# Attention scores of the first query block as one product for both halves of the keys, and the mask added on VectorE

## The chip, the cores and the metric

The kernel runs on one core of one Trainium2 chip. The metric is the device time of one execution in microseconds (us); less is better. The median of three runs of the kernel before is 2488.39 us.

## The reference

Two layers of a streaming encoder work on 256 frames of width 2048. Layer 0 mixes tokens with a gated spatial MLP, layer 1 with latent attention of 16 heads; behind each stands a gated MLP with a short causal convolution. The change is in the attention of layer 1. Queries come in blocks of 128, and a block reads keys up to its own end. A frame sees keys of its own chunk of 64 frames and of earlier ones:

```python
for qb in range(S // Q_BLOCK):
    q0 = qb * Q_BLOCK
    k_end = q0 + Q_BLOCK
    s = (jnp.einsum('bqhd,bkhd->bhqk', q_nope[:, q0:k_end], k_nope[:, :k_end])
         + jnp.einsum('bqhr,bkr->bhqk', q_rope[:, q0:k_end], k_rope[:, :k_end]))
    s = s.astype(jnp.float32) * SM_SCALE
    allowed = (kpos[None, :] // CHUNK) <= (qpos[:, None] // CHUNK)
    s = jnp.where(allowed[None, None], s, -jnp.inf)
    p = jax.nn.softmax(s, axis=-1).astype(v.dtype)
    outs.append(jnp.einsum('bhqk,bkhd->bqhd', p, v[:, :k_end]))
```

So the first block has scores of 128 queries by 128 keys, the second of 128 by 256. In each, the first 64 queries of the block must not see the last 64 of its keys.

## The kernel before

**Precision by halves.** TensorE multiplies rounded operands (type fp32r). For the precision of fp32 each operand is split into a rounded part, called high, and the rest, called low. ScalarE makes the high part (a cast: `wh` of a weight, line 127, `hi` of an activation), VectorE the low part (a subtraction: `wl`, line 130). A product is then high x high + low x high + high x low, added up in a PSUM bank. The class `Feed` loads weights in chunks of 128x2048 by DMA from SyncE's queue and splits them ahead of their use; its casts stand on ScalarE and VectorE between all other work.

**One head, in three steps.** `attend_a` (line 1059) makes the scores `sc` of one head in one PSUM bank: columns 0 to 127 for the first block of queries, 128 to 383 for the second. Per block there are five products: high queries by high keys, low queries by high keys, high queries by low keys (`knT`, `qnT`), and two of the rotary part (`krT`, whose two halves lie side by side, with `qrT`). The mask is an eleventh product: `negq` has -1e30 in row 0 for the first 64 queries, `keyr` has 1 in row 0 for the last 64 keys of each block, and their product, of 256 columns in bf16, adds -1e30 where a key is hidden. Then VectorE takes the maximum of each block (line 1079, out of PSUM) and scales it (1080), ScalarE takes the exponentials with their sums (1082), VectorE the reciprocal (1084) and the scaled probabilities `p` (1086).

`attend_b` (line 1089) transposes `p` in three products into `pt` (1094), and ScalarE copies it to `pts` (1096). `attend_c` (line 1099) multiplies by the values `vv` into `o` and splits that into `oT`: ScalarE the high part (1108), VectorE the low one (1109).

**The loop over heads** (lines 1135 to 1154) weaves these steps of three heads into the output projection `mo`. Heads 0 to 3 get their scores earlier, between the products that make `vv`. An iteration `t` has, on TensorE, the scores of head t; six `mo` products of 512 columns for the first 128 frames (`acc[0]`); the transposes of head t-1; three `mo` products; the values of head t-2; three more `mo` products. `mo` of iteration t uses the head `t - 4`.

**What sets the order.** Each engine runs its instructions in order and waits on semaphores of others. The Tile framework schedules: it may move an instruction past others of the same engine, so the order on an engine is not the source's. Eight PSUM banks are shared: four hold `mo`, four go around among `sc`, `pt` and `o`.

Of the kernel before, what the change touches and what calls it, by code (L numbers as in the profile page):

```python
# [8 lines left out]
F32 = mybir.dt.float32  # L9
F32R = mybir.dt.float32r  # L10
BF16 = mybir.dt.bfloat16
AF = mybir.ActivationFunctionType
ALU = mybir.AluOpType
AX = mybir.AxisListType

P = 128
S = 256
D = 2048
KD = D // P
# [5 lines left out]
H = 16  # L25
# [5 lines left out]
SM_SCALE = (NOPE + ROPE) ** -0.5  # L31
LN_EPS = 1e-5
RMS_EPS = 1e-6
NEG = -1.0e30
# [17 lines left out]
T1, T2 = 6, 5  # L52
# [161 lines left out]
def trunk(ctx: ExitStack, tc: tile.TileContext, x, xT, gm_in, gm_wout, ffn_up, ffn_dn,  # L214
          ml_q, ml_kv, ml_b, ml_out, consts, w_sT, b_s, ropes, ln_rows, out):
    nc = tc.nc

    cpool = ctx.enter_context(tc.tile_pool(name="cpool", bufs=1))
    big = ctx.enter_context(tc.tile_pool(name="big", bufs=1))
    tp = ctx.enter_context(tc.tile_pool(name="tp", bufs=3))  # L220
# [6 lines left out]
    def slot(shape, name, dt=F32, tag="big"):  # L227
        return big.tile(shape, dt, tag=tag, name=name, bufs=SLOTS[tag])
# [4 lines left out]
    def mm(o, l, r, start, stop):  # L233
        recent[0] = nc.tensor.matmul(o, l, r, start=start, stop=stop, skip_group_check=True)  # L234
# [70 lines left out]
    for j in range(4):  # L305
        t = slot([P, 4, S], f"xraw{j}", tag="side")
# [35 lines left out]
    nc.gpsimd.memset(epsc[:, 0:1], LN_EPS)  # L342
    nc.gpsimd.memset(epsc[:, 1:2], RMS_EPS)

    negq = cpool.tile([P, P], BF16, name="negq")
    nc.gpsimd.memset(negq, 0.0)
    nc.gpsimd.memset(negq[0:1, 0:64], NEG)
    keyr = cpool.tile([P, 2, P], BF16, name="keyr")
    nc.gpsimd.memset(keyr, 0.0)
    nc.gpsimd.memset(keyr[0:1, :, 64:P], 1.0)  # L350

    def rstd_of(var, eps, name):
        q = st.tile([P, 1], F32, tag="rstd", name=f"{name}q")
# [6 lines left out]
    def x_parts(xs, k, b):  # L360
        t = xs[k // 4]
        return (t[:, k % 4, b * P : (b + 1) * P], t[:, k % 4, S + b * P : S + (b + 1) * P])

    def prod_b(acc, parts, hi, lo, pieces, first, last):

        xh, xl = parts
        for f, (o, w) in enumerate(pieces):
            mm(acc[f][:, :w], xh, hi[:, o : o + w], first, False)
            mm(acc[f][:, :w], xl, hi[:, o : o + w], False, False)
            mm(acc[f][:, :w], xh, lo[:, o : o + w], False, last)  # L370
# [322 lines left out]
    halfp = [(0, 512), (512, 512)]  # L693
# [15 lines left out]
    for gi in range(6):  # L709

        acc = Banks(f"v{gi}", DIRECT if gi == 0 else DIRECT + OWN if gi % 2 else OWN + DIRECT)
# [23 lines left out]
        for i, (n, t) in enumerate(zip(DIRECT, rest)):  # L735
            o = vt[:, i // 2, (i % 2) * 512 : (i % 2) * 512 + 512]
# [75 lines left out]
    for gi in range(12):  # L812
        acc = [bank(f"u{gi}_{f}") for f in range(4)]
        for c in range(4):
            hi, lo = feed.next()
# [14 lines left out]
    acc, end = down(NF_GM, pT, "wo", ln, acts)  # L830
# [69 lines left out]
    ln, acc, end = ffn(0, ln, acc, end, False)  # L900
# [5 lines left out]
    krT = slot([P, 2, S], "krT", F32R)  # L906
# [55 lines left out]
    acc = [[bank(f"mkv{b}_{f}") for f in range(2)] for b in range(2)]  # L962
    for c in range(6):
        hi, lo = feed.next()
        for j in range(3 if c < 5 else 1):
            k = 3 * c + j
# [9 lines left out]
    for b in range(2):  # L976
# [3 lines left out]
        t = tp.tile([P, 4, ROPE], F32, tag="t1", name=f"kr2_{b}", bufs=T1)  # L980
# [13 lines left out]
    qrT = [slot([P, 8, S], f"qrT{i}", F32R) for i in range(2)]  # L994
# [4 lines left out]
    acc = [[bank(f"qr{b}_{f}") for f in range(2)] for b in range(2)]  # L999
    for c in range(2):  # L1000
        hi, lo = feed.next()
        for j in range(2):
            k = 2 * c + j
# [52 lines left out]
    oT = []  # L1056
    probs = {}

    def attend_a(h):

        q, k = qT[h // 4][:, h % 4, :], kT[h // 4][:, h % 4, :]
        sc = bank(f"sc{h}")
        mx = st.tile([P, 4, 2], F32, tag="mx", name=f"mx{h}")
        p = tp.tile([P, 3 * P], F32, tag="t2", name=f"p{h}", bufs=T2)
        cc = [slice(0, P), slice(P, 3 * P)]
        for b in range(2):
            nk = (b + 1) * P
            o = sc[:, cc[b]]

            qh, ql = q[:, b * P : (b + 1) * P], q[:, S + b * P : S + (b + 1) * P]  # L1070
            qr = qrT[h // 8][:, h % 8, b * P : (b + 1) * P]
            mm(o, qh, k[:, 0:nk], b == 0, False)
            mm(o, ql, k[:, 0:nk], False, False)
            mm(o, qh, k[:, S : S + nk], False, False)
            mm(o, qr, krT[:, 0, 0:nk], False, False)
            mm(o, qr, krT[:, 1, 0:nk], False, False)
        mm(sc.rearrange("p (n c) -> p n c", n=2)[:, :, 0:P], negq, keyr, False, True)
        for b in range(2):
            nc.vector.reduce_max(mx[:, 0, b : b + 1], sc[:, cc[b]], axis=AX.X)
        nc.vector.tensor_scalar(mx[:, 1, :], mx[:, 0, :], -SM_SCALE, None, op0=ALU.mult)  # L1080
        for b in range(2):
            nc.scalar.activation(p[:, cc[b]], sc[:, cc[b]], AF.Exp, bias=mx[:, 1, b : b + 1], scale=SM_SCALE,
                                 accum_out=mx[:, 2, b : b + 1])
        nc.vector.reciprocal(mx[:, 3, :], mx[:, 2, :])
        for b in range(2):
            nc.vector.tensor_scalar(p[:, cc[b]], p[:, cc[b]], mx[:, 3, b : b + 1], None, op0=ALU.mult)
        probs[h] = p
# [11 lines left out]
    def attend_c(h):  # L1099
        if h % 4 == 0:  # L1100
            oT.append(slot([P, 4, 512], f"oT{h // 4}", F32R))
        pts = probs.pop(h)
        o = bank(f"o{h}")
        c = slice(h * P, (h + 1) * P)
        mm(o[:, 0:S], vv[0][:, c], pts[:, 0:S], True, False)
        mm(o[:, P:S], vv[1][:, c], pts[:, S : 3 * P], False, True)
        hi = oT[h // 4][:, h % 4, 0:S]
        nc.scalar.copy(hi, o[:, 0:S])
        nc.vector.tensor_tensor(oT[h // 4][:, h % 4, S : 2 * S], o[:, 0:S], hi.bitcast(F32), ALU.subtract)  # L1109

    for hf in range(2):
        acc = [[bank(f"vv{hf}_{b}_{f}") for f in range(2)] for b in range(2)]
        for c in range(2):
            hi, lo = feed.next()
            for j in range(2):

                k = 2 * c + j
# [7 lines left out]
        for b in range(2):  # L1125
            for f in range(2):
                c = slice(hf * 1024 + f * 512, hf * 1024 + (f + 1) * 512)
# [4 lines left out]
    acc = [[bank(f"mo0_{b}_{f}") for f in range(2)] for b in range(2)]  # L1132
    LAG = 4
    attend_c(0)
    for t in range(3, H + LAG):
        k = t - LAG
        if k >= 0:
            if k % 2 == 0:
                hi, lo = feed.next()
            w = slice((k % 2) * 1024, (k % 2) * 1024 + 1024)  # L1140
        if 3 < t < H:
            attend_a(t)
        if k >= 0:
            prod_b(acc[0], x_parts(oT, k, 0), hi[:, w], lo[:, w], halfp, k == 0, k == KD - 1)
        if t == 3:
            attend_c(1)
        if t - 1 < H:
            attend_b(t - 1)
        if k >= 0:
            prod_b(acc[1][:1], x_parts(oT, k, 1), hi[:, w], lo[:, w], halfp[:1], k == 0, k == KD - 1)  # L1150
        if 3 < t < H + 2:
            attend_c(t - 2)
        if k >= 0:
            prod_b(acc[1][1:], x_parts(oT, k, 1), hi[:, w], lo[:, w], halfp[1:], k == 0, k == KD - 1)
    ln.begin()
# [4 lines left out]
    acc = [[bank(f"mo1_{b}_{f}") for f in range(2)] for b in range(2)]  # L1160
    late = []
    for c in range(8):
        left = 7 - c
        hi, lo = feed.next(splits=2 if left > 5 else 3, loads=2)
        for j in range(2):
            k = 2 * c + j
            w = slice(j * 1024, (j + 1) * 1024)
# [11 lines left out]
    ln, acc, end = ffn(1, ln, banks, end_mo, True)  # L1179
# [92 lines left out]
```

## Time and profile before

| what | value |
|---|---|
| median of 3 runs | 2488.39 us (2487.24 to 2489.69) |
| profiled execution | 2486.63 us |
| its span | 2484.8 us |
| TensorE busy | 2468.0 us, 99% |
| VectorE busy | 1992.9 us, 80% |
| ScalarE busy | 1424.6 us, 57% |
| scores of the 16 heads | between 1626 and 1709 us of the span |

The span is what the profiler saw between first and last instruction; the execution's own time is 1.8 us longer. PE is TensorE's matrix part, PEld its loads of weights, DVE is VectorE, ACT ScalarE, POOL GpSimd, SP SyncE. Matmuls overlap and their ends are modelled: how long one really costs is seen from its start to the start of the next.

### The profile page before, as it was taken

The page shows a single profiled execution, that of the slowest core. Times are in us where ns is not written, and L with a number is a line of the kernel's source. Part 1 is how long each engine was busy: PE and PEld are TensorE (multiplying, and loading weights), DVE is VectorE, ACT ScalarE, POOL GpSimd, SP SyncE. Part 2 cuts the span into 40 slices and gives each one's busy share as a digit, 9 for nine tenths or more (in the row PEclk, how much of TensorE's full clock was granted, in tenths as well). Part 3 has the DMA queues.
Part 4 walks back from the last instruction along what each step waited for, and adds up shares of the span by engine and source line. Part 5 has one row for each costly group of instructions (what it writes and reads, how often), then busy time and mean ns, then how long its engine had stood idle before and what let it go on. Part 6 is the DMA issues. An engine that isn't in the chain of part 4 may idle for free. (4 is left out here: it accounts for less than half of the span.)

```text
span 2484.8 us, 33520 instructions
## 1 busy us (share of the span) xinstructions
PE 2468.0 (99%) x12995; PEld 2122.3 (85%) x12995; DVE 1992.9 (80%) x2802; ACT 1424.6 (57%) x1979; POOL 89.0 (4%) x173
## 2 busy tenths in 40 slices
PE   9999999999999999999999999999999999999998
PEld 7888888888888888888888888988888888888886
DVE  7999866679898789787677897856598788768798
ACT  6676544446565756566554566655566656655453
POOL 0000000000000000000000000000001000000000
PEclk9999999999999999999999999999999999999999
DMA  7556544546665689788558885544489789647885
GB/s 280 203 206 223 198 173 169 185 170 214 209 203 203 218 349 351 286 335 315 188 198 319 302 305 185 182 155 151 174 294 347 293 333 341 238 155 286 299 325 199
DMA packets 108991, 606.17 MB, mean 244 GB/s; under 512 B 10272, under 2 KB 11040, under 8 KB 61600
## 3 DMA queue, kind: packets, MB, share of 16 engines
q1 hardware_dynamic: 84832, 463.51, 52.2%
q0 software_dynamic: 24000, 140.52, 14.7%
q8 instruction: 102, 1.67, 0.3%
q14 instruction: 57, 0.47, 0.1%
HBM read 538.98 MB, written 65.01 MB: 243 GB/s over the span
## 5 line engine op out<-in xcount | busy, mean ns | idle before, releaser
L130 DVE TENSOR_TENSOR wl<-raw,wh 128x1024 fp32r<-128x1024 f32 (+4 forms) x693 | 968.2, 1418 | 222.4 <-ACT wh L127 136.9
L127 ACT CAST wh<-raw 128x1024 fp32r<-128x1024 f32 (+4 forms) x693 | 820.2, 1211 | 388.0 <-PE u L234 84.6
L234 PE MATMUL up<-xhl,wh 128*128 128x512 f32 x2624 | 612.0, 390 | 0.9 <-ACT wh L127 0.9
L234 PEld LDWEIGHTS up<-xhl,wh 128*128 128x128 f32 x2624 | 487.3, 188 | 99.4 <-ACT wh L127 1.8
L234 PEld LDWEIGHTS up<-xhl,wl 128*128 128x128 f32 x2624 | 325.9, 192 | 7.2 <-DVE wl L130 0.7
L234 PE MATMUL up<-xhl,wl 128*128 128x256 f32 x2624 | 328.5, 283 | 0.5 <-DVE wl L130 0.5
L234 PE MATMUL u<-xhl,wh 128*128 128x512 f32 x768 | 184.7, 393 | 0.1
L234 PEld LDWEIGHTS u<-xhl,wh 128*128 128x128 f32 x768 | 141.0, 188 | 31.6 <-issue 3.8
L127 ACT CAST th<-ts 128x1536 fp32r<-128x1536 f32 x106 | 110.1, 1052 | 87.8 <-DVE ts L137 62.7
L130 DVE TENSOR_TENSOR tl<-ts,th 128x1536 fp32r<-128x1536 f32 x106 | 125.3, 1218 | 8.1 <-PE dn_p L234 3.4
L234 PEld LDWEIGHTS u<-xhl,wl 128*128 128x128 f32 x768 | 95.4, 192 | 2.0
L234 PE MATMUL u<-xhl,wl 128*128 128x256 f32 x768 | 96.0, 283 | 0.0
L234 PE MATMUL mo<-wh,oT 128*128 128x512 f32 x256 | 83.0, 404 | 0.0
L137 DVE TENSOR_TENSOR ts<-ts,raw 128x512 f32<-128x512 f32 x106 | 72.6, 685 | 0.9
L234 PE MATMUL v_q<-wh,xhl 128*128 128x512 f32 x224 | 69.2, 390 | 1.2 <-ACT wh L127 1.2
L137 DVE TENSOR_TENSOR ts<-raw 128x1024 f32<-128x1024 f32 x53 | 64.5, 1218 | 0.9 <-PE wo_q L234 0.7
L234 PE MATMUL v_p<-wh,xhl 128*128 128x512 f32 x192 | 59.8, 390 | 0.1
L234 PEld LDWEIGHTS mo<-wh,oT 128*128 128x128 f32 x256 | 45.4, 189 | 7.4 <-DVE oT L1109 0.2
L234 PEld LDWEIGHTS v_q<-wh,xhl 128*128 128x128 f32 x224 | 41.9, 188 | 10.7 <-ACT wh L127 2.1
L234 PE MATMUL mo<-wl,oT 128*128 128x512 f32 x128 | 50.2, 392 | 0.0
L686 ACT ACTIVATE lny<-lnt,lncol 128x128 f32<-128x128 f32 x96 | 36.6, 471 | 15.6 <-PE lnt L682 15.5
L171 DVE TENSOR_TENSOR pwl<-praw,pwh 128x1536 fp32r<-128x1536 f32 x16 | 28.1, 1755 | 20.4 <-ACT pwh L170 20.4
(1701 smaller groups left out, 4165.4 us busy)
## 6 DMA issues: line engine op xcount, KB each, us to landing
raw<-in_ffn_up_dram SPq DMA_DIRECT2D x172, 1024.0 KB, 6.4
raw<-in_gm_in_dram SPq DMA_DIRECT2D x93, 1024.0 KB, 4.8
raw<-in_ffn_dn_dram SPq DMA_DIRECT2D x68, 1024.0 KB, 6.8
raw<-in_gm_wout_dram SPq DMA_DIRECT2D x48, 1024.0 KB, 5.4
praw<-in_ffn_dn_dram POOLq DMA_DIRECT2D x16, 1024.0 KB, 14.8
keptth<-pth POOLq DMA_DIRECT2D x16, 1024.0 KB, 6.4
kepttl<-ptl POOLq DMA_DIRECT2D x16, 1024.0 KB, 8.8
fth<-keptth POOLq DMA_DIRECT2D x16, 1024.0 KB, 9.5
```

What stands on the lines that cost most here:

```text
L127: cast = self.nc.scalar.copy(hi, raw)
L130: self.nc.vector.tensor_tensor(lo, raw, hi.bitcast(F32), ALU.subtract)
L137: add = lambda o, a, b: self.nc.vector.tensor_tensor(o, a, b, ALU.add)
L171: pin(nc.vector.tensor_tensor(lo[:, 0:cols], raw[:, o : o + cols], hi[:, 0:cols].bitcast(F32), ALU.subtract))
L234: recent[0] = nc.tensor.matmul(o, l, r, start=start, stop=stop, skip_group_check=True)
L686: nc.scalar.activation(y[:, j], t[:, j * P : (j + 1) * P], AF.Identity, bias=lncol[:, o : o + 1], scale=lncol[:, g : g + 1])
```

## The change

For the first block of queries, three products take the place of five: high queries by high and low keys side by side in one product of 256 columns (a view of two blocks of 128), low queries by high keys (128 columns), and the rotary queries by both halves of the rotary keys (256 columns). The two halves of the result lie in columns 0 to 127 and 128 to 255; ScalarE copies the second to SBUF (`sl`, line 1079 of the changed kernel), and VectorE adds it to the first into `p` (1082). The second block of queries has the five products that it had, in columns 256 to 511. The mask product goes: VectorE adds a column `negc` (-1e30 in its first 64 rows) in place to the two hidden groups of 64 columns (1081). Maximum and exponential of the first block read `p` in SBUF instead of PSUM. In the loop, `attend_c` of head t-2 moves ahead of `attend_b` of head t-1, and that behind three more `mo` products.

```diff
--- before.py
+++ after.py
@@ -342,12 +342,9 @@
     nc.gpsimd.memset(epsc[:, 0:1], LN_EPS)
     nc.gpsimd.memset(epsc[:, 1:2], RMS_EPS)
 
-    negq = cpool.tile([P, P], BF16, name="negq")
-    nc.gpsimd.memset(negq, 0.0)
-    nc.gpsimd.memset(negq[0:1, 0:64], NEG)
-    keyr = cpool.tile([P, 2, P], BF16, name="keyr")
-    nc.gpsimd.memset(keyr, 0.0)
-    nc.gpsimd.memset(keyr[0:1, :, 64:P], 1.0)
+    negc = cpool.tile([P, 1], F32, name="negc")
+    nc.gpsimd.memset(negc, 0.0)
+    nc.gpsimd.memset(negc[0:64, :], NEG)
 
     def rstd_of(var, eps, name):
         q = st.tile([P, 1], F32, tag="rstd", name=f"{name}q")
@@ -1063,23 +1060,32 @@
         mx = st.tile([P, 4, 2], F32, tag="mx", name=f"mx{h}")
         p = tp.tile([P, 3 * P], F32, tag="t2", name=f"p{h}", bufs=T2)
         cc = [slice(0, P), slice(P, 3 * P)]
+        two = lambda t: t.rearrange("p (n c) -> p n c", n=2)
+        qh = lambda b: q[:, b * P : (b + 1) * P]
+        ql = lambda b: q[:, S + b * P : S + (b + 1) * P]
+        qr = lambda b: qrT[h // 8][:, h % 8, b * P : (b + 1) * P]
+
+        mm(two(sc[:, 0:S]), qh(0), two(k)[:, :, 0:P], True, False)
+        mm(sc[:, 0:P], ql(0), k[:, 0:P], False, False)
+        mm(two(sc[:, 0:S]), qr(0), krT[:, :, 0:P], False, False)
+        o = sc[:, S : 2 * S]
+        mm(o, qh(1), k[:, 0:S], False, False)
+        mm(o, ql(1), k[:, 0:S], False, False)
+        mm(o, qh(1), k[:, S : 2 * S], False, False)
+        mm(o, qr(1), krT[:, 0, :], False, False)
+        mm(o, qr(1), krT[:, 1, :], False, True)
+
+        lo = tp.tile([P, P], F32, tag="t1", name=f"sl{h}", bufs=T1)
+        nc.scalar.copy(lo, sc[:, P:S])
+        hidden = sc.rearrange("p (n c) -> p n c", c=64)[:, 1:8:6, :]
+        nc.vector.tensor_scalar(hidden, hidden, negc, None, op0=ALU.add)
+        nc.vector.tensor_tensor(p[:, cc[0]], sc[:, 0:P], lo, ALU.add)
+        src = [p[:, cc[0]], o]
         for b in range(2):
-            nk = (b + 1) * P
-            o = sc[:, cc[b]]
-
-            qh, ql = q[:, b * P : (b + 1) * P], q[:, S + b * P : S + (b + 1) * P]
-            qr = qrT[h // 8][:, h % 8, b * P : (b + 1) * P]
-            mm(o, qh, k[:, 0:nk], b == 0, False)
-            mm(o, ql, k[:, 0:nk], False, False)
-            mm(o, qh, k[:, S : S + nk], False, False)
-            mm(o, qr, krT[:, 0, 0:nk], False, False)
-            mm(o, qr, krT[:, 1, 0:nk], False, False)
-        mm(sc.rearrange("p (n c) -> p n c", n=2)[:, :, 0:P], negq, keyr, False, True)
-        for b in range(2):
-            nc.vector.reduce_max(mx[:, 0, b : b + 1], sc[:, cc[b]], axis=AX.X)
+            nc.vector.reduce_max(mx[:, 0, b : b + 1], src[b], axis=AX.X)
         nc.vector.tensor_scalar(mx[:, 1, :], mx[:, 0, :], -SM_SCALE, None, op0=ALU.mult)
         for b in range(2):
-            nc.scalar.activation(p[:, cc[b]], sc[:, cc[b]], AF.Exp, bias=mx[:, 1, b : b + 1], scale=SM_SCALE,
+            nc.scalar.activation(p[:, cc[b]], src[b], AF.Exp, bias=mx[:, 1, b : b + 1], scale=SM_SCALE,
                                  accum_out=mx[:, 2, b : b + 1])
         nc.vector.reciprocal(mx[:, 3, :], mx[:, 2, :])
         for b in range(2):
@@ -1142,14 +1148,12 @@
             attend_a(t)
         if k >= 0:
             prod_b(acc[0], x_parts(oT, k, 0), hi[:, w], lo[:, w], halfp, k == 0, k == KD - 1)
-        if t == 3:
-            attend_c(1)
+        if t < H + 2:
+            attend_c(t - 2)
+        if k >= 0:
+            prod_b(acc[1][:1], x_parts(oT, k, 1), hi[:, w], lo[:, w], halfp[:1], k == 0, k == KD - 1)
         if t - 1 < H:
             attend_b(t - 1)
-        if k >= 0:
-            prod_b(acc[1][:1], x_parts(oT, k, 1), hi[:, w], lo[:, w], halfp[:1], k == 0, k == KD - 1)
-        if 3 < t < H + 2:
-            attend_c(t - 2)
         if k >= 0:
             prod_b(acc[1][1:], x_parts(oT, k, 1), hi[:, w], lo[:, w], halfp[1:], k == 0, k == KD - 1)
     ln.begin()
```

What the scheduler makes of it. First a steady iteration on TensorE, with the scores of head 9. Before, its score products:

```order
L234 MATMUL sc_14726<-knT_14109,qnT_13809 128x128 x3
L234 MATMUL sc_14726<-krT,qrT_13464 128x128 x2
L234 MATMUL sc_14726<-knT_14109,qnT_13809 128x256 x3
L234 MATMUL sc_14726<-krT,qrT_13464 128x256 x2
L234 LDWEIGHTS negq
L234 MATMUL sc_14726<-keyr,negq 128x2x128
```

and now:

```order
L234 MATMUL sc_14732<-knT_14106,qnT_13806 128x256
L234 MATMUL sc_14732<-knT_14106,qnT_13806 128x128
L234 MATMUL sc_14732<-krT,qrT_13461 128x256
L234 MATMUL sc_14732<-knT_14106,qnT_13806 128x256 x3
L234 MATMUL sc_14732<-krT,qrT_13461 128x256 x2
```

Eleven products are eight. Behind the scores come, before and after, four rows of `mo_0` (six products). What follows these was:

```order
L1094 MATMUL pt_14754<-ident,p_14683 128x128 x3
L234 MATMUL mo_1_0_14457<-wh_14476,oT_14619 128x512 x2
L234 MATMUL mo_1_0_14457<-wl_14477,oT_14619 128x512
L234 MATMUL o_14763<-pts_14713,vv_13465 128x256
L234 MATMUL o_14763<-pts_14713,vv_13466 128x128
L234 MATMUL mo_1_1_14458<-wh_14476,oT_14619 128x512 x2
L234 MATMUL mo_1_1_14458<-wl_14477,oT_14619 128x512
```

and is now:

```order
L234 MATMUL o_14761<-pts_14727,vv_13462 128x256
L234 MATMUL o_14761<-pts_14727,vv_13463 128x128
L234 MATMUL mo_1_0_14458<-wh_14477,oT_14614 128x512 x2
L234 MATMUL mo_1_0_14458<-wl_14478,oT_14614 128x512
L1100 MATMUL pt_14769<-ident,p_14688 128x128 x3
L234 MATMUL mo_1_1_14459<-wh_14477,oT_14614 128x512 x2
L234 MATMUL mo_1_1_14459<-wl_14478,oT_14614 128x512
```

The values `o` of head 7 stood behind the transposes `pt` of head 8; now they stand ahead of them, and three `mo` products more stand ahead of `pt`. On ScalarE the same iterations (heads 8 and 9) had:

```order
L1108 CAST oT_14619<-o_14718 128x256
L1082 ACTIVATE p_14683,mx_14682<-sc_14681,mx_14682 128x128
L1082 ACTIVATE p_14683,mx_14682<-sc_14681,mx_14682 128x256
L1096 COPY pts_14713<-pt_14709 128x384
L1082 ACTIVATE p_14728,mx_14727<-sc_14726,mx_14727 128x128
L1082 ACTIVATE p_14728,mx_14727<-sc_14726,mx_14727 128x256
L1096 COPY pts_14758<-pt_14754 128x384
L1108 CAST oT_14619<-o_14763 128x256
```

and have now:

```order
L1079 COPY sl_14697<-sc_14686 128x128
L1114 CAST oT_14614<-o_14715 128x256
L1102 COPY pts_14727<-pt_14723 128x384
L1088 ACTIVATE p_14688,mx_14687<-p_14688,mx_14687 128x128
L1088 ACTIVATE p_14688,mx_14687<-sc_14686,mx_14687 128x256
L1079 COPY sl_14743<-sc_14732 128x128
L1114 CAST oT_14614<-o_14761 128x256
L1088 ACTIVATE p_14734,mx_14733<-p_14734,mx_14733 128x128
```

The copy `pts` of head 7, which stood behind the exponentials of head 8, stands ahead of them, right behind the cast of `oT`. So it is for most heads; for heads 4, 5 and 8 the copy still stands behind the next head's exponentials.

Second, ScalarE where the loop begins. `pts` here is the copy for head 2, `vv` are the copies of the values. Before:

```order
L1128 COPY vv_13465<-vv_0_0_14327 128x512
L1128 COPY vv_13465<-vv_0_1_14328 128x512
L1128 COPY vv_13466<-vv_1_0_14329 128x512
L1128 COPY vv_13466<-vv_1_1_14330 128x512
L1108 CAST oT_14459<-o_14460 128x256
L1108 CAST oT_14459<-o_14465 128x256
L1096 COPY pts_14474<-pt_14470 128x384
L127 CAST wh_14476<-raw_14337 128x1024 x2
L1082 ACTIVATE p_14486,mx_14485<-sc_14484,mx_14485 128x128
```

and now:

```order
L1134 COPY vv_13462<-vv_0_0_14326 128x512
L1134 COPY vv_13462<-vv_0_1_14327 128x512
L1134 COPY vv_13463<-vv_1_0_14328 128x512
L1134 COPY vv_13463<-vv_1_1_14329 128x512
L1114 CAST oT_14460<-o_14461 128x256
L127 CAST wh_14477<-raw_14336 128x1024
L1114 CAST oT_14460<-o_14466 128x256
L1102 COPY pts_14475<-pt_14471 128x384
L127 CAST wh_14477<-raw_14336 128x1024
L1088 ACTIVATE p_14419,mx_14418<-p_14419,mx_14418 128x128
```

Half of a pair of casts `wh` has moved ahead of the copy.

Third, VectorE at head 15, the last. Before:

```order
L1079 TENSOR_REDUCE mx_15023<-sc_15022 128x1
L1109 TENSOR_TENSOR oT_15013<-o_15014,oT_15013 128x256
L1079 TENSOR_REDUCE mx_15023<-sc_15022 128x1
L130 TENSOR_TENSOR wl_15068<-raw_14876,wh_15067 128x1024
L1080 TENSOR_SCALAR mx_15023<-mx_15023 128x2
L130 TENSOR_TENSOR wl_15068<-raw_14876,wh_15067 128x1024
L1084 RECIPROCAL mx_15023<-mx_15023 128x2
L1086 TENSOR_SCALAR p_15024<-p_15024,mx_15023 128x128
L1086 TENSOR_SCALAR p_15024<-p_15024,mx_15023 128x256
```

and now:

```order
L1081 TENSOR_SCALAR sc_15034<-sc_15034,negc 128x2x64
L130 TENSOR_TENSOR wl_15081<-raw_14885,wh_15080 128x1024
L1082 TENSOR_TENSOR p_15036<-sc_15034,sl_15045 128x128
L1085 TENSOR_REDUCE mx_15035<-sc_15034 128x1
L1085 TENSOR_REDUCE mx_15035<-p_15036 128x1
L1115 TENSOR_TENSOR oT_15016<-o_15063,oT_15016 128x256
L1086 TENSOR_SCALAR mx_15035<-mx_15035 128x2
L130 TENSOR_TENSOR wl_15081<-raw_14885,wh_15080 128x1024
L130 TENSOR_TENSOR wl_15129<-raw_14985,wh_15128 128x1024
L1090 RECIPROCAL mx_15035<-mx_15035 128x2
L130 TENSOR_TENSOR wl_15129<-raw_14985,wh_15128 128x1024
L1092 TENSOR_SCALAR p_15036<-p_15036,mx_15035 128x128
L1092 TENSOR_SCALAR p_15036<-p_15036,mx_15035 128x256
```

Between the head's first own step and its scaling there were two casts `wl`, now there are four.

## Prediction

> **What bounds the kernel now.** I begin with the page, to see which engine the span belongs to.
>
> ```profile
> span 2484.8 us, 33520 instructions
> PE 2468.0 (99%) x12995; PEld 2122.3 (85%) x12995; DVE 1992.9 (80%) x2802; ACT 1424.6 (57%) x1979; POOL 89.0 (4%) x173
> ```
>
> TensorE (PE) is busy in 99% of the span. That is an average over stages, and modelled ends can hide small gaps, so I take the stage that is changed, in the view of stretches. Its columns are the stretch, its length, then busy time of PE, weight loads, VectorE, ScalarE and GpSimd, then the granted clock.
>
> ```profile
> 1680.00:1690.00 10.00, 10.00 (x61) 8.67 (x60) 6.04 (x16) 5.21 (x15) 0.00 (x0) 1.00 0.32 107
> 1690.00:1700.00 10.00, 10.00 (x61) 8.69 (x60) 6.04 (x17) 5.46 (x17) 0.00 (x0) 1.00 0.30 105
> ```
>
> PE has no idle time, VectorE and ScalarE have four to five us in ten, the clock is at full. The view of waits says the same: for 1620 to 1725 us, in which all 16 heads run, it has no wait of a product, and of the weight loads only these two.
>
> ```profile
> PEld vv L234 <- ACT qrT L1029: 0.3, 1, 0.3
> PEld mo L234 <- DVE oT L1109: 0.2, 1, 0.2
> ```
>
> So here time is the sum of what PE issues, and a product taken away is time taken away unless a new wait takes its place. Does a gain last until the end? In the whole execution the products waited for other engines' work as little as this (the rest of that view is 1.7, 1.3 and 1.2 us, all before this stage):
>
> ```profile
> PE up L234 <- ACT wh L127: 0.9, 2, 0.5
> PE up L234 <- DVE wl L130: 0.5, 1, 0.5
> ```
>
> PE stays the bound behind the stage, so I let the gain arrive whole.
>
> **What PE loses.** The chain that ended last gives the true cost per head, since it runs from release to release. One iteration of the loop over heads:
>
> ```profile
> 1671.59 1.27 PE sc L234 x11
> 1672.86 1.39 PE mo L234 x6
> 1674.25 0.33 PE pt L1094 x3
> 1674.58 0.70 PE mo L234 x3
> 1675.28 0.66 PE o L234 x4
> 1675.94 0.70 PE mo L234 x3
> 1676.64 1.27 PE sc L234 x11
> 1677.91 1.39 PE mo L234 x6
> 1679.30 0.33 PE pt L1094 x3
> ```
>
> The eleven score products cost 1.27 us of the 5.05 us that a head takes. How this splits shows in the order of time, by start to start (the second column is the modelled length and overlaps):
>
> ```profile
> 1686.56 0.44 PE L234 MATMUL sc<-knT,qnT 128*128 128x128 f32 x3
> 1686.84 0.39 PE L234 MATMUL sc<-krT,qrT 128*128 128x128 f32 x2
> 1687.06 0.56 PE L234 MATMUL sc<-knT,qnT 128*128 128x256 f32 x3
> 1687.47 0.40 PE L234 MATMUL sc<-krT,qrT 128*128 128x256 f32 x2
> 1687.70 0.28 PE L234 MATMUL sc<-keyr,negq 128*128 128x256 bf16 x1
> ```
>
> Five products of 128 columns took 0.50 us (1686.56 to 1687.06), about 0.10 to 0.11 each. Two of 256 columns took 0.23 (1687.47 to 1687.70), 0.118 each. The mask product is what is left of 1.27: 0.13. A short product thus costs nearly what a long one does. Before there are five short, five long and the mask; after, one short and seven long. Seven by 0.118 and one by 0.11 is 0.94, so a head saves **0.33 us**. Ends: with the mean of all five long ones (0.64/5 = 0.128) the new block is 1.00 and the saving 0.27; at one price for all (1.27/11 = 0.115) three products fewer are 0.35. Sixteen heads: 16 x 0.33 = **5.3 us**, ends 4.3 and 5.6.
>
> [...]
>
> **What VectorE and ScalarE gain.** Per head a copy on ScalarE (sl, 128x128 out of PSUM), on VectorE the mask (two blocks of 64 columns, in place in PSUM) and the sum of the halves. The first reduction and exponential read SBUF instead of PSUM. None of the three is in this trace. The nearest rows (count, then busy us and mean ns):
>
> ```profile
> L1096 ACT COPY pts<-pt 128x384 f32<-128x384 f32 x16 | 7.8, 488 | 0.0
> L1082 ACT ACTIVATE p<-sc,mx 128x128 f32<-128x128 f32 x16 | 5.9, 371 | 17.6 <-DVE mx L1080 17.6
> L1109 DVE TENSOR_TENSOR oT<-o,oT 128x256 fp32r<-128x256 f32 x16 | 6.7, 421 | 6.6 <-ACT oT L1108 6.6
> L1079 DVE TENSOR_REDUCE mx<-sc 128x1 f32<-128x256 f32 x16 | 6.6, 414 | 0.0
> L1079 DVE TENSOR_REDUCE mx<-sc 128x1 f32<-128x128 f32 x16 | 4.6, 285 | 5.9 <-PE sc L234 5.9
> L1086 DVE TENSOR_SCALAR p<-p,mx 128x128 f32<-128x128 f32 x16 | 4.6, 286 | 0.5
> L130 DVE TENSOR_TENSOR wl<-raw,wh 128x1024 fp32r<-128x1024 f32 x28 | 33.1, 1221 | 15.1 <-ACT wh L127 14.1 <-PE sc L234 0.9
> ```
>
> The two reductions differ by 0.13 us for 128 columns. So the sum of halves is 0.42 - 0.13 = 0.29, the mask like the 128-column rows 0.29 (ends of both 0.27 and 0.42), the copy 0.27 (ends 0.2 and 0.37). These are estimates from these rows. VectorE's load grows by 2 x 0.58 us in some ten: from 6.0 to 7.2. It is not the bound, and the casts (wl, wh) keep room. What counts is the **delay**: the mask waits for the copy, the sum for the mask, the maximum of the first block for the sum, and the transposes pt wait behind all of them.
>
> How much room is there? The worst steady head is the one whose scores begin at 1671.59: two casts of wl stand ahead of its maximum. Its probabilities and the weight load of its transposes:
>
> ```profile
> 1677.81 0.55 DVE L1086 TENSOR_SCALAR p<-p,mx 128x128 f32<-128x128 f32 x2
> 1678.91 0.48 PEld L1094 LDWEIGHTS pt<-ident,p 128*128 128x128 f32 x3
> ```
>
> The scaling ends at 1678.36, the load starts at 1678.91: 0.55 us to spare. The new order gives more: one o (0.66) and one group of three mo products (0.70) more come between a head's scores and its pt, and the scores of the next head are 0.33 shorter: +1.03. The delay costs about 0.3 for the copy with its hand-over, 0.33 for the mask with its own, 0.2 for the sum, whose end overlaps with the other reduction: -0.83. That leaves 0.75, so PE does not wait in the steady iterations. Heads 3, 5 and 7 get one or two casts between their scores and their scaling. A head with none ahead takes this long now:
>
> ```profile
> 1686.72 1.27 PE sc L234 x11
> 1690.45 0.55 DVE L1086 TENSOR_SCALAR p<-p,mx 128x128 f32<-128x128 f32 x2
> ```
>
> From 1687.99 to 1691.00 is 3.0 us; with 0.83 and two casts of 1.22 it is 6.3, and the room is 1678.91 - 1672.86 + 1.03 = 7.1. They fit too.
>
> In the other window, from pt to o, the room shrinks: 0.70 + 0.94 + 1.39 = 3.0 us, where it was 0.70 + 0.66 + 0.70 + 1.27 + 1.39 + 0.33 + 0.70 = 5.75. It holds one copy of 0.49, and that copy has run late:
>
> ```profile
> 1677.47 0.47 ACT L1096 COPY pts<-pt 128x384 f32<-128x384 f32 x1
> ```
>
> The transposes for it ended at 1674.58, so it began 2.9 us behind them, since ScalarE had the exponentials of the next head ahead of it. At that place it would be too late now. But in the new order it stands in most heads ahead of those exponentials, right behind the cast of oT, and 3.0 us suffice.
>
> **Two places where it does not fit.** First, head 2, where the loop begins: o of this head moves ahead of ten other products, and on ScalarE one cast of wh (row below, half of the pair) gets in front of the copy that it needs. Nothing to one whole cast; I take 0.4 us.
>
> ```profile
> 1691.55 1.99 ACT L127 CAST wh<-raw 128x1024 fp32r<-128x1024 f32 x2
> ```
>
> Second, head 15: four casts of wl (1.22 each) stand between its mask and its scaling, where there were two between maximum and scaling. Part of them runs while VectorE waits for the exponentials anyway, and the scheduler put its pt later too. Nothing to one cast; I take 0.4. The wait of 0.2 that mo has now for oT at the loop's start goes. Together 0.6 us lost, ends 0 and 2.3.
>
> **Sum.** 5.3 - 0.6 = 4.7 us less. The profiled execution took 2486.63, which makes 2481.9; its span and the 1.8 us around it change alike. It lay 1.76 under the median of the runs, 2488.39, so for the median I forecast **2483.7 us**, 0.19% less. Ends of this case: 5.6 + 0.2 less is 2482.6, 4.3 - 2.3 less is 2486.4.
>
> **Rivals.** (a) *Columns are the price.* If the short products only look dear because their neighbours' weights come late, what is saved is 256 columns a head (2176 before, 1920 after). By the chain's row, six of 512 columns in 1.39 us, these are 0.115 us: 1.8 in all, less 0.6, is 2487.2. [...] Against it stands 0.50 us for five short products, in every head. (b) *Half is given back.* In every second iteration VectorE does the two casts just ahead of the mask, and pt waits as long as a head saves: 8 x 0.33 = 2.6 more, 2486.3. For it: the new operations are unmeasured, and the margin is 0.75. With 0.42 for both VectorE operations and 0.37 for the copy it falls to about 0.4, still positive. (c) *Slower: the casts come between.* If in those eight iterations the pair of casts (2 x 1.22) delays a head's scaling as well as its mask, pt waits 2.44 - 0.75 = 1.7 us there: 13.5 more, 2488.4 - 4.7 + 13.5 = 2497.2. Its place is pt's weight load, and it decides once the delay is over 0.83 + 0.75 = 1.6 us, twice my estimate. Against it: from head 8 to head 14 the new order has the casts behind the scaling of one head and ahead of the mask of the next, never between. (d) *It does not do what it says* would need the products to be as many as before; the order shows eight.
>
> **Chances.** My forecast 0.70, (a) 0.09, (b) 0.14, (c) 0.07. About 0.2% (5 us) is what a measurement of this kernel can tell from no change; 4.98 us less lies inside my own case, between the 4.7 taken and the 5.8 without any wait: I put 0.36 of its 0.70 beyond it. So faster 0.36; same 0.34 + 0.09 + 0.14 = 0.57; slower 0.07. The range has the ends of my case, (a) and (b), and the spread of single runs around a median (1.2 us): 2481.6 to 2487.8. It leaves out (c) and some edges.
>
> **What would show it.** Right: in the chain the score block is eight products in 0.92 to 1.00 us; an iteration takes 4.7 us instead of 5.05; the waits of weight loads have pt and o once each near the loop's start and end, under half a us. Wrong: a block of 1.15 us speaks for (a); waits of pt for VectorE in each second iteration speak for (b), of over 1 us for (c); the mask or the sum at over 0.42 us, or ScalarE's copy late behind casts, breaks the margin; a new wait of up or dn products behind the stage would show that the gain was lost later.

## Result and profile after

| | before | with the change |
|---|---|---|
| median | 2488.04 us (2485.65 to 2492.37, 7 runs) | 2480.97 us (2479.13 to 2483.06, 7 runs) |
| ratio of the times | | 0.9976, 95% interval 0.9966 to 0.9985 |
| profiled execution, its span | 2486.63, 2484.8 us | 2481.38, 2479.3 us |

By the ratio the change saves 6.0 us, with an interval of 3.7 to 8.5. So the kernel is faster by 0.24%, between 0.15 and 0.34%. I forecast 4.7 us, 0.19%, just under the 0.2% that I had taken as the least that can be told from no change, and thought "same" likelier (0.57) than "faster" (0.36). The interval lies clear of zero, but it holds 0.2%.

First the page's head: fewer products, VectorE busier.

```profile
span 2479.3 us, 33472 instructions
PE 2463.7 (99%) x12947; PEld 2117.2 (85%) x12947; DVE 1999.7 (81%) x2834; ACT 1428.6 (58%) x1995; POOL 88.4 (4%) x171
```

TensorE has 48 products fewer in this list (three for each head). In the stage, the view of stretches has PE still without idle time, and VectorE at 7.35 us in ten where it was at 6.04:

```profile
1680.00:1690.00 10.00, 10.00 (x59) 8.65 (x58) 7.35 (x21) 5.98 (x17) 0.00 (x0) 1.00 0.31 107
```

The chain through one iteration, from scores to scores:

```profile
1676.93 0.94 PE sc L234 x8
1677.88 1.39 PE mo L234 x6
1679.26 0.65 PE o L234 x4
1679.91 0.69 PE mo L234 x3
1680.60 0.33 PE pt L1100 x3
1680.93 0.69 PE mo L234 x3
1681.62 0.94 PE sc L234 x8
```

The block of scores has gone from 1.27 to 0.94 us, the iteration from 5.05 to 4.69. Nothing else in it has changed by more than 0.01. The block in order of time, in which a product's price is the distance between starts:

```profile
1681.46 0.34 PE L234 MATMUL sc<-knT,qnT 128*128 128x256 f32 x2
1681.64 0.33 PE L234 MATMUL sc<-krT,qrT 128*128 128x256 f32 x1
1681.81 0.52 PE L234 MATMUL sc<-knT,qnT 128*128 128x256 f32 x3
1682.17 0.40 PE L234 MATMUL sc<-krT,qrT 128*128 128x256 f32 x2
1682.41 0.63 PE L234 MATMUL mo<-wh,oT 128*128 128x512 f32 x2
```

Five long products from 1681.81 to 1682.41 are 0.12 us each. The first block's three end 0.35 us after their start (1681.46 to 1681.81), where five took 0.50.

How much did the stage gain? The view of one tile gives first and last start of its products. From the first score product to the last product of `mo`, before:

```profile
L234 PE MATMUL sc<-knT,qnT x96: 218/277/336, 1626.5 to 1707.5; 128*128 128x128 f32 x48, 128*128 128x256 f32 x48
...
L234 PE MATMUL mo<-wl,oT x128: 387/389/401, 1653.0 to 1768.2; 128*128 128x512 f32 x128
```

and now:

```profile
L234 PE MATMUL sc<-knT,qnT x80: 220/280/362, 1625.0 to 1700.8; 128*128 128x256 f32 x64, 128*128 128x128 f32 x16
...
L234 PE MATMUL mo<-wl,oT x128: 387/389/479, 1650.7 to 1761.6; 128*128 128x512 f32 x128
```

That is 141.7 us before (1768.2 - 1626.5) and 136.6 now: **5.1 us** less. The table below has this for every run. I call "ahead" what lies before the first score product, and "behind" the span's rest after the last `mo` product.

| kernel | score products per head | their block, us | iteration, us | stage, us | ahead, us | behind, us |
|---|---|---|---|---|---|---|
| before | 11 | 1.27 | 5.05 | 141.7 | 1626.5 | 716.6 |
| with the change | 8 | 0.94 | 4.69 | 136.6 | 1625.0 | 717.7 |
| the change again | 8 | 0.94 | 4.69 | 136.6 | 1625.2 | 717.3 |
| old loop order | 8 | 0.94 to 0.96 | 4.73 and more | 137.7 | 1627.7 | 718.4 |
| loop order only | 11 | 1.27 | 5.03 | 141.5 | 1625.2 | 719.8 |
| mask only | 10 | 1.15 | 4.89 | 139.3 | 1626.2 | 717.1 |
| merge only | 9 | 1.07 | 4.83 | 138.1 | 1625.0 | 715.9 |
| short products of 64 columns | 11 | 1.27 | 5.03 | 141.6 | 1625.0 | 717.3 |
| short products of 256 columns | 11 | 1.31 | 5.07 | 142.1 | 1626.1 | 718.6 |
| 64 weight columns, mask first | 11 | 1.07 | 4.85 | 138.2 | 1624.3 | 716.7 |
| 64 weight and 64 key columns | 11 | 1.06 | 4.83 | 138.0 | 1627.0 | 715.8 |
| mask first | 11 | 1.28 | 5.05 | 141.6 | 1625.5 | 717.4 |
| sum three times | 8 | 0.94 | uneven | 137.9 | 1628.1 | 715.5 |
| sum five times | 8 | 0.95 | uneven | 141.8 | 1625.4 | 720.2 |

The iteration is that of one head; neighbours differ by up to 0.02 us (before: 5.03 and 5.05 by turns). In the two profiles of the changed kernel the stage is the same to 0.1 us, ahead and behind to 0.4. From kernel to kernel ahead moves by 3.8 us and behind by 4.7, although nothing was changed in them. Whether that belongs to a kernel or to an execution, single profiles don't tell. Totals of one kernel spread by 4 to 8 us. So the stage of one profile tells more of a change of 5 us than a single total does.

### The profile page after: what moved, and what is told of

Read it like the earlier page. It is cut to its first block, busy times and chain, and to the rows that moved or that the text cites. A ratio compares the mean times of both kernels' runs of the same rounds, so it can differ in the third digit from the quotient of the medians.

```text
span 2479.3 us, 33472 instructions
## 1 busy us (share of the span) xinstructions
PE 2463.7 (99%) x12947; PEld 2117.2 (85%) x12947; DVE 1999.7 (81%) x2834; ACT 1428.6 (58%) x1995; POOL 88.4 (4%) x171
```

## Experiments

**Which part carries the gain?** Four kernels separate the new products, the mask and the order of the loop.

*The new products with the old loop order.*

```diff
-        if t < H + 2:
-            attend_c(t - 2)
+        if t == 3:
+            attend_c(1)
+        if t - 1 < H:
+            attend_b(t - 1)
...
-        if t - 1 < H:
-            attend_b(t - 1)
+        if 3 < t < H + 2:
+            attend_c(t - 2)
```

> The changed kernel with the loop over heads as it was before (transposes, three mo products, values, three mo products). Theory, the products carry the gain and the loop order only keeps it whole: the score block stays 0.94 us, and from the first score product to the last mo product the stage takes 137.9 to 138.4 us (136.6 with the whole change, 141.7 before), since the transposes lose room. In the heads that had 0.55, 0.61 and 0.96 us to spare, 0.33 of a shorter score block and 0.9 of a later scaling (mask measured at 0.36) leave waits of 0.68, 0.62 and 0.27; heads with 1.4 or more wait for nothing. Time about 2483.5. Rival, the loop order carries the gain: the transposes wait in each second iteration by what a head saves or more, the stage is 140 us or longer, time 2486 or more.

Measured: median 2483.74 us (11 runs; before, in the same set, 2486.02), ratio 0.9986 (0.9977 to 0.9995). The stage is 137.7 us, 1.1 longer than with the whole change and 0.2 under the range that I expected. The transposes' loads wait in heads 5, 7 and 8 too, where they had room:

```profile
PEld pt L1100 <- issue: 1.1, 3, 0.6
...
PEld pt L1100 <- ACT sl L1079: 0.4, 1, 0.4
PEld pt L1100 <- DVE p L1092: 0.4, 1, 0.4
```

The products carry the gain: 4.0 of the stage's 5.1 us come without the new loop order. The order saves the other 1.1. In six iterations, from 1651 to 1680 us, the scheduler put `pt` at other places than the source does, so 1.1 is the price of the old order as the scheduler mends it.

*The new loop order alone.*

```diff
-        if t == 3:
-            attend_c(1)
+        if t < H + 2:
+            attend_c(t - 2)
...
```

> The kernel before with the new loop order alone (11 score products, mask as a product). Theory: TensorE issues the same products and waited for nothing, so iterations stay 5.04 and the stage 141.5 to 141.9 us, the time within 1 us of before. Rival, moving the values ahead of the transposes gains by itself: a stage under 141 us.

Measured: ratio 1.0005 (0.9996 to 1.0014), stage 141.5 us. By itself the order is worth next to nothing, 0.2 us of stage. It gives room that only the new chain needs.

*Only the mask moved to VectorE* (and the new loop order).

```diff
-            mm(o, qr, krT[:, 1, 0:nk], False, False)
-        mm(sc.rearrange("p (n c) -> p n c", n=2)[:, :, 0:P], negq, keyr, False, True)
+            mm(o, qr, krT[:, 1, 0:nk], False, b == 1)
+        hidden = sc.rearrange("p (n c) -> p n c", c=64)[:, 1:6:4, :]
+        nc.vector.tensor_scalar(hidden, hidden, negc, None, op0=ALU.add)
```

> The kernel before with the new loop order and with the mask added by VectorE; the ten other score products as before. Theory, the mask product costs what is left of its block, 0.12 to 0.13 us, although the next product starts 0.04 behind its own start (the product behind it comes 0.085 later than usual): iteration 4.92, stage 139.3 to 139.8 us, time 2 us under before. Rival, it hid behind its neighbours: iteration 5.04, stage 141.5. Other rival, the mask's 0.36 us on VectorE brings waits of the transposes: more than 0.5 us of them in the stage.

Measured: ratio 0.9991 (0.9982 to 1.0000), stage 139.3 us. No load for the transposes or values waits. In the kernel before, the product behind the mask's began 0.04 us after it (1687.70, in the prediction's rows):

```profile
1687.74 0.71 PE L234 MATMUL mo<-wh,oT 128*128 128x512 f32 x2
1688.29 0.40 PE L234 MATMUL mo<-wl,oT 128*128 128x512 f32 x1
```

and with the mask on VectorE the same two products of `mo` are:

```profile
1685.80 0.63 PE L234 MATMUL mo<-wh,oT 128*128 128x512 f32 x2
1686.27 0.39 PE L234 MATMUL mo<-wl,oT 128*128 128x512 f32 x1
```

They take 0.47 us instead of 0.55. So of the 0.12 us that the block loses, two thirds, 0.08, stood in the products that followed the mask's.

*Only the merged products* (new loop order, the mask a product).

```diff
-        mm(o, qr(1), krT[:, 1, :], False, True)
+        mm(o, qr(1), krT[:, 1, :], False, False)
+        mm(sc.rearrange("p (n c) -> p n c", c=P)[:, 0:4:3, :], negq, keyr, False, True)
...
-        nc.vector.tensor_scalar(hidden, hidden, negc, None, op0=ALU.add)
```

> The changed kernel with the mask as a product again (over the same columns), nine score products, no mask on VectorE. Theory, a 128-column product costs nearly what a 256-column one does, so five for three saves 0.21 us a head: iteration 4.82, stage 138.0 to 138.6 us, time 3.5 us under before. Rival, columns are the price (640 of them before, 640 now): iteration 5.0 and stage above 141 us.

Measured: ratio 0.9988 (0.9979 to 0.9997), stage 138.1 us. The chain shows nine products in 1.06 to 1.07 us:

```profile
1677.93 1.06 PE sc L234 x9
...
1682.75 1.07 PE sc L234 x9
```

The number of columns is 2176 as before, the block is 0.20 us shorter. Columns are not the price. Measured from the kernel with the loop order alone (141.5), the mask saves 2.2 us of stage and the merge 3.4. Together that would be 5.6. The whole change saves 4.9 from there. The missing 0.7 fits the waits of heads 2 and 15 (0.64 us of products, below), which neither part has alone.

**What is the price of a short product?** Four kernels change the sizes of the five products of the first block in the kernel before.

*Half the columns* (the first block's scores for its last 64 keys are left out).

```diff
+            nn = nk if b else 64
+            o = o[:, 0:nn]
-            mm(o, qh, k[:, 0:nk], b == 0, False)
+            mm(o, qh, k[:, 0:nn], b == 0, False)
...
```

> The kernel before with its five first-block products over 64 columns instead of 128 (the scores of the first block for its last 64 keys are left out; the mask product still covers these columns). Theory, a short product has a floor that does not depend on its columns, about 0.11 us: iteration 5.04 as before (5.00 to 5.05). Rival, columns are the price (512 in 0.23 us, 0.45 ns each): 320 columns fewer are 0.14 us, iteration 4.90.

Measured: one run, 2485.72 us; the block is still 1.27 us long.

```profile
1675.16 1.27 PE sc L234 x11
1680.19 1.27 PE sc L234 x11
```

From block to block 5.03 us: 64 columns cost what 128 do.

*Twice the columns* (scores that nobody reads).

```diff
-            o = sc[:, cc[b]]
+            o = sc[:, b * S : (b + 1) * S]
-            mm(o, qh, k[:, 0:nk], b == 0, False)
+            mm(o, qh, k[:, 0:S], b == 0, False)
...
```

> The kernel before with its five first-block products over 256 columns (the scores of keys that the first block doesn't read are computed too and not used; the second block lies in columns 256 to 511). Theory of the floor: each of the five goes from 0.11 to 0.118, iteration 5.07 to 5.10. Rival, columns are the price: 640 columns more are 0.29 us, iteration 5.33.

Measured: one run, 2488.69 us; block 1.31, iteration 5.07. 640 columns more cost 0.04 us in the block and 0.02 to 0.03 in the iteration, far from the rival's 0.29.

*Half the weights* (the first block's last 64 queries are left out), mask first.

```diff
+        mm(sc.rearrange("p (n c) -> p n c", n=2)[:, :, 0:P], negq, keyr, True, False)
...
+            qq = P if b else 64
+            o = o[0:qq]
-            mm(o, qh, k[:, 0:nk], b == 0, False)
+            mm(o, qh[:, 0:qq], k[:, 0:nk], False, False)
...
```

> The kernel before with 64 instead of 128 queries as the weights of the five first-block products (the first block's last 64 queries are left out), and the mask product first in the block. What makes the floor? If it is the load of 128 weight columns, five loads of half the size save up to 5 x 0.05 = 0.27 us, iteration 4.8 to 4.9. If it is a fixed price of a product, whatever it loads, the iteration stays 5.02 to 5.05.

Measured: one run, 2481.06 us; iteration 4.85, stage 138.2 us. In order of time, the two rotary products of the first block and what follows:

```profile
1682.20 0.29 PE L234 MATMUL sc<-krT,qrT 128*64 128x128 f32 x2
1682.32 0.57 PE L234 MATMUL sc<-knT,qnT 128*128 128x256 f32 x3
```

Two products with 64 weight columns take 0.12 us, 0.06 each; with 128 they took 0.22 (1686.84 to 1687.06 in the prediction's rows), 0.11 each. The 0.05 us a load in the expectation was my estimate; what is measured is 0.05 less for each of these two products. Two more runs belong to it.

*The control, the mask first and everything in full size.*

```diff
+        mm(sc.rearrange("p (n c) -> p n c", n=2)[:, :, 0:P], negq, keyr, True, False)
...
-            mm(o, qh, k[:, 0:nk], b == 0, False)
+            mm(o, qh, k[:, 0:nk], False, False)
...
-        mm(sc.rearrange("p (n c) -> p n c", n=2)[:, :, 0:P], negq, keyr, False, True)
```

> A control for the run with 64 queries as weights: the kernel before with the mask product first in its block, all products in full size. Theory, the place of the mask product is worth next to nothing: iteration 5.00 to 5.05, stage 141.0 to 141.7 us. Rival, the 0.20 us a head that the run with 64 queries saved came from this move: iteration 4.85, stage 138.3.

Measured: one run, 2486.36 us; iteration 5.05, stage 141.6 us. The place of the mask product is worth nothing, so the 0.20 us a head come from the smaller weights.

*Half the weights and half the columns.* (The last 64 keys are left out for the first block as well.)

```diff
-            o = o[0:qq]
+            nn = nk if b else 64
+            o = o[0:qq, 0:nn]
...
```

> As the run with 64 queries as weights (mask product first, the first block's last 64 queries left out), and its five first-block products over 64 columns as well (the scores for the last 64 keys are left out too). There five short products took 0.06 us each, which fits a load of 64 weight columns at half the price of 128, but also 128 columns at 0.45 ns (0.058). Theory, the load of weights is what is left: iteration 4.83 to 4.85 as there. Rival, columns are now the price: 5 x 0.029 = 0.14 less, iteration 4.70.

Measured: one run, 2482.65 us; iteration 4.83, block 1.06 against 1.07. Even with half the weights the columns don't decide. What sets the pace of these short products here is the number of weight columns: the block takes 1.28 us with 128 (mask first) and 1.07 with 64. The runs don't separate the load itself from the narrower output that goes with it.

**How much delay does VectorE's chain bear?** The sum is written again, with the same result.

```diff
         nc.vector.tensor_tensor(p[:, cc[0]], sc[:, 0:P], lo, ALU.add)
+        nc.vector.tensor_tensor(p[:, cc[0]], sc[:, 0:P], lo, ALU.add)
+        nc.vector.tensor_tensor(p[:, cc[0]], sc[:, 0:P], lo, ALU.add)
```

> The changed kernel with the sum of the halves written three times over (same result), 2 x 0.287 = 0.57 us more in each head's chain on VectorE. The profile of the changed kernel leaves the transposes 0.42 to 0.65 us in heads 12, 7, 8 and 5, nothing in heads 3 and 15, and 0.8 or more in the others. Theory, the room is what decides: waits of 0.57 in heads 3 and 15 and at most 0.15 in a few others, stage 137.5 to 138.5 us (136.6 without). Rival (a), VectorE is busy 7 us in 10 and has slack: stage within 0.2 us of 136.6. Rival (b), each head pays: 16 x 0.57 = 9.1, stage 145.

Measured: one run, 2483.51 us; stage 137.9 us, 1.3 more for 0.57 us of delay in each head. Slack of the engine would give 0, a price for each head 9.1; the sum by room, 137.5 to 138.5, holds. The places don't: loads of `pt` wait 0.8 us in head 0 and 0.3 to 0.5 in heads 3, 6, 7, 8, 9 and 15, where I expected hardly anything outside 3 and 15. The scheduler also moved products: in some heads `pt` stands behind other products of `mo` than before. So this run shows what the delay costs after the scheduler's answer to it, and that the room of each head decides is argued. With five sums, written as two more such lines:

> The changed kernel with the sum written five times over (same result), 4 x 0.287 = 1.15 us more in each head's chain. Theory, past the room of 0.42 to 1.0 us that most heads have: waits of 0.1 to 0.75 in heads 4, 5, 7, 8, 10, 12 and 14 and of 1.15 in heads 3 and 15, in all about 5.5 us, stage 141 to 143.5 us: the whole gain is spent, as long as before (141.7). Rival (a), slack: 136.6 to 137. Rival (b), each head pays: 16 x 1.15 = 18, stage 155.

Measured: one run, 2489.46 us; stage 141.8 us, as expected. The whole gain is gone; the scheduler moved `pt` further still, behind up to 24 products of `mo`, and the loads wait for the probabilities and for ScalarE's copies:

```profile
PEld pt L1104 <- issue: 2.3, 3, 1.5
PEld o L234 <- ACT pts L1106: 2.2, 4, 0.8
PEld pt L1104 <- DVE p L1096: 1.8, 1, 1.8
```

**What lies outside the stage?** The change once more.

> The changed kernel once more, for what lies outside its stage. Theory: the stage is 136.6 us again; the wait of 1.7 us of wo_q for h_u before the stage, which the first profile of before had and that of the changed kernel had not, and the waits of up for wl behind it come and go from run to run in both kernels, as no instruction there was changed. Rival: the change itself removes the one and brings the others, then they are as in its first profile: no wait of wo_q of over 0.5, and 1.4 us for wl. Time 2479 to 2483 either way.

Measured: median 2480.59 us (9 runs; before, in the same set, 2486.05), ratio 0.9976 (0.9966 to 0.9986); stage 136.6 us. Outside the stage I compare the waits of weight loads. Before:

```profile
PEld wo_q L234 <- DVE h_u L393: 1.9, 1, 1.9
...
PEld up L234 <- DVE wl L130: 0.7, 1, 0.7
```

With the change:

```profile
PEld up L234 <- DVE wl L130: 2.1, 3, 1.0
...
PEld wo_q L234 <- DVE h_u L390: 0.3, 1, 0.3
```

The change once more:

```profile
PEld up L234 <- DVE wl L130: 1.6, 2, 0.9
...
PEld wo_q L234 <- DVE h_u L390: 0.5, 1, 0.5
```

I had expected these waits to come and go in one kernel. They did not: the second profile of the change looks like its first, as the rival had it. Other kernels speak against the rival. The long wait of `wo_q` is there with the new products and the old loop order (1.8) and with the sum written three times (1.9), and it is missing from two kernels without the new products, the new loop order alone (0.6) and the mask first (0.2). So it doesn't go with the new products, and a large wait for `wl` (3.8 with the new loop order alone) doesn't either. Whether such waits belong to a kernel as it is built or to an execution stays open, and with it whether the changed kernel gains something outside its stage each time.

In the first pair of profiles, ahead gave 1.5 us, the stage 5.1, and behind took 1.1: the span's 5.5. Only the middle one is shown to be the change's.

## Why the prediction was right, and where it was off

**The products: right to the digit.** The block was to be 0.94 us and is 0.94; sixteen heads by 0.33 are 5.3 us. The reason held too: a 128-column product costs nearly what a 256-column one costs (0.11 and 0.12 us from start to start), since the price of these short products goes with the number of weight columns: about 0.11 us from product to product with 128 and 0.06 with 64, though the runs don't show the load by itself. (The prediction's 0.10 to 0.11 us for a short product is a little high for its first three, which take 0.28 us, 0.093 each.) Rival (a), that columns are the price, fell with the first profile (it asked for a block of 1.15 us) and again with the run of 64 columns.

**The new operations: one of three too cheap.** The view of groups of the changed kernel, between 1620 and 1725 us, has (count, then busy us and mean ns) the exponential of the first block, the mask, the sum and the copy:

```profile
L1088 ACT ACTIVATE p<-p,mx 128x128 f32<-128x128 f32 x16 | 6.5, 406 | 7.3 <-DVE mx L1086 7.3
...
L1081 DVE TENSOR_SCALAR sc<-sc,negc 128x128 f32<-128x128 f32 x16 | 5.7, 356 | 5.0 <-ACT sl L1079 4.9
...
L1082 DVE TENSOR_TENSOR p<-sc,sl 128x128 f32<-128x128 f32 x16 | 4.6, 287 | 0.2
...
L1079 ACT COPY sl<-sc 128x128 f32<-128x128 f32 x16 | 4.3, 268 | 2.7 <-PE sc L234 2.7
```

Copy 0.27 (estimate 0.27), sum 0.29 (0.29), mask 0.36 (0.29; the bounds of 0.27 to 0.42 held). I had priced the mask like the scaling of `p`, which reads and writes SBUF; the mask works in PSUM. The exponential that I left at 0.37 takes 0.41, now that its source is SBUF.

The rows of the mask and of the scaling differ by 70 ns (356 against 286 for the scaling of `p` of 128 columns, quoted in the prediction). No run tests whether PSUM is the cause: the mask also lies in two blocks of 64. And not every operation is much dearer from PSUM: the maximum over 128 columns takes 285 ns from there (before) and 276 from SBUF (now), and the exponential, on ScalarE, takes 371 from PSUM (before) and 406 from SBUF (now).

**The room of the transposes: the delay was mis-sized, and that nothing waited was in part luck.** I forecast 0.75 us to spare in the worst steady head, which is head 8. It has 0.57. Head 12 has the least now, in order of time:

```profile
1693.33 0.54 DVE L1092 TENSOR_SCALAR p<-p,mx 128x128 f32<-128x128 f32 x2
...
1694.29 0.48 PEld L1100 LDWEIGHTS pt<-ident,p 128*128 128x128 f32 x3
```

The scaling ends at 1693.87, the load begins at 1694.29: 0.42 us. The mask's 0.07 and the exponential's 0.04 don't explain it. The term that failed is the delay of 0.83 us, which I took to be the same for every head. The prediction's head with no casts ahead, head 11, took 3.0 us from the end of its scores to the end of its scaling. Now its scores end at 1682.56 (the chain above), and VectorE has:

```profile
1683.39 0.55 DVE L1092 TENSOR_SCALAR p<-p,mx 128x128 f32<-128x128 f32 x2
...
1684.19 0.35 DVE L1081 TENSOR_SCALAR sc<-sc,negc 128x128 f32<-128x128 f32 x1
...
1687.28 0.55 DVE L1092 TENSOR_SCALAR p<-p,mx 128x128 f32<-128x128 f32 x2
```

The last row is its scaling. It ends at 1687.83, 5.3 us behind the scores: 2.3 us more than before, not 0.83. The first row is the scaling of head 10, and the mask of head 11 stands behind it, 1.6 us behind the scores, where my sum had 0.3 for the copy. (The copy itself begins only at 1683.31, behind the exponentials of head 10 on ScalarE.) I had counted what the chain of one head gets longer. But the chain got longer and the iteration shorter, so the chains of two heads now overlap on these engines, and one stands behind the other. With the mask alone or the merged products alone head 11 keeps 4.0 us of room; with both it has 1.77.

Nothing waited in a steady iteration all the same, so rivals (b) and (c), half given back and slower, did not come. But that rested on room that I had not counted: head 11 had 3.03 us to spare before, head 12 had 1.53, and the new order added the 1.03 that I had counted. My check of the worst head was too narrow, and the forecast held there partly by luck.

How near was a loss? With 0.57 us more in each head's chain the stage lost 1.3 us, with 1.15 more 5.2, as much as was gained. With 0.42 us in head 12, the change lies nearer to that than the 0.75 of the forecast. The old loop order, which takes room away, lost 1.1.

**The room of the values: right.** The copy `pts` was to come early enough in a window of 3.0 us. In most steady heads it ends 2.07 us before it is read (for head 11 at 1690.89 and 1692.96), in the tightest, head 14, 0.83.

**The two places: named rightly, a little overpriced.** In the stage only these loads wait, beside one of `vv` that stood there before:

```profile
PEld o L234 <- ACT pts L1102: 0.8, 2, 0.5
PEld pt L1100 <- issue: 0.4, 1, 0.4
...
PEld pt L1100 <- DVE p L1092: 0.2, 1, 0.2
```

Loads stand idle for 1.4 us there, but the products lose less. The chain shows it, for head 2 and around head 15:

```profile
1649.86 0.04 issue
1649.90 0.70 PE o L234 x2
...
1651.53 0.22 PE o L234 x2
...
1709.63 0.30 PE pt L1100
...
1710.17 0.22 PE pt L1100 x2
...
1711.09 0.79 PE o L234 x4
```

For head 2 the four products of `o` take 0.92 us where 0.65 is usual, with the 0.04 ahead 0.31 lost (I took 0.4). For head 15 `pt` takes 0.52 instead of 0.33 and `o` 0.79 instead of 0.65, 0.33 lost (0.4; that part of it would be at `o` I had not said). Less the 0.2 of `mo` that went, it is 0.4 to 0.5 where I had 0.6. The rest of the stage's 5.1 us are hundredths: groups of `mo` and `o` that are 0.01 shorter, as in the run with the loop order alone.

**The time.** The stage saved 5.1 us where I forecast 4.7. The ratio gives 6.0 with an interval that holds both. The 0.9 between 5.1 and 6.0 is not explained, and can't be from these runs. It is in fact 0.2 larger: the time around the span, which the prediction took to stay at 1.8 us, was 1.8 to 1.9 in the runs of before and 2.0 to 2.1 in those of the change, so 0.2 us of the stage's gain don't reach the total. Against the median of 2488.39 on which I built, the ratio gives 2482.4, inside my range; the median that was measured, 2480.97, lies 0.6 under its lower end. What failed there is the spread: I allowed 1.2 us around a median (and took only 1.0 of it off at the lower end, 2482.6 to 2481.6), but the median of before itself was 2488.04, 2486.02 and 2486.05 in three sets of runs, and the 2488.39 came from three runs of the first. On which side of 0.2% the change lies, 0.15 to 0.34% does not decide. Rivals (a) and (b), at 0.05 and 0.08%, lie outside it.

## What to carry to other kernels

When products of 128 columns with 128 weight columns stand in a row, count products, not columns (here 0.11 us for one, and 0.12 for one of 256 columns): put two that share their weights side by side in one of 256 columns, and let another engine add the halves. First see in the chain that TensorE never waits there, and then count the room of the chain that gets longer, in every head and together with the chain of the head before it on the same engine, since past that room the gain goes (here 1.15 us more in each head's chain cost 5.2 us of stage, as much as was gained). Where the change is smaller than the spread of the total, measure the stage from its first product to its last.

## What the runs showed of the hardware

- A product of 64, 128 and 256 columns with 128 weight columns in fp32r costs 0.11, 0.11 and 0.12 us from start to start (the two rotary products of a block; the three ahead of them take 0.08 and 0.09 each over 64 and 128 columns, 0.12 over 256); one of 512 columns 0.23. With 64 weight columns a rotary product takes 0.06, over 128 and over 64 columns.
- The price of a product can stand in the one behind it: the mask's product began 0.04 us ahead of the next, and the block lost 0.12 without it, 0.08 of this in the products behind it.
- An operation of VectorE on 2 x 64 columns in PSUM, in place, takes 356 ns; the scaling of 128 columns in SBUF 286. The maximum over 128 columns takes 285 ns from PSUM and 276 from SBUF. The exponential of 128 columns takes 406 ns from SBUF and 371 from PSUM.
- In the changed stage loads of weights wait for 1.4 us, and its products lose 0.6.
